# A Strassen-type trunk kernel: the first stage begins with two plain float32 products, and sums, transposes and the end are reordered

## The chip, the cores and the metric

The kernel runs on 1 core of a Trainium2 chip. The metric is the device time of one execution in microseconds (us). The core has five engines that run their own queues in order: TensorE (PE in the rows; its weight loads are PEld), VectorE (DVE), ScalarE (ACT), GpSimd (POOL) and SyncE (SP), which here issues the DMAs. TensorE's clock has two levels, 1.2 and 2.4 GHz; the rows give the granted clock as a share of the higher.

## The reference

One decoder layer on x of 2048 tokens by 1024 features, then a final norm. Cut to what matters:

```
def reference(x, mem, ...):
    x = x + hybrid_mixer(rms_norm(x, g_mix), w_in, ...)          # 1024 -> 3072 columns, attention and short
                                                                 # convolution, norms of both, w_out
    x = x + memory_cross_attention(rms_norm(x, g_xattn), rms_norm(mem, g_mem), ...)
    x = x + squared_relu_mlp(rms_norm(x, g_mlp), w_up, w_down)   # 1024 -> 4096 -> 1024
    return rms_norm(x, g_final)

def rms_norm(x, g):
    return x * rsqrt(mean(x * x, axis=-1) + 1e-6) * g
```

Everything is float32.

## The kernel before

The large products run in stages `g` of 28 steps. A stage multiplies a 1024 x 1024 weight block by 1024 tokens in the scheme of Strassen and Winograd: seven products of 512 x 512 quadrants in the order (1, 2, 6, 7, 4, 5, 3), each in four steps `m`, one for 128 output rows (or, for the values of attention, two steps of 2 x 128 tokens with the operands exchanged). Stage -2 ("vg") is the first: the values and the gate of the first 1024 tokens. Its product 1 is weight quadrant (0,0) by x quadrant (0,0), product 2 is quadrant (0,1) by (1,0); product 6 is the first that needs sums of quadrants.

A product is computed from split operands: ScalarE rounds an operand to float32r (`w_hi` for weights, `o_hi` for activations), VectorE subtracts that from the original (`w_lo`, `o_lo`), and TensorE multiplies high by high, low by high and high by low, three products of 128 x 128 x 512 for each of four k (`mlp_mm`, L370 to L395). In the first stage `o_hi` also scales by `g_mix`, and the row norm is applied to the results. `o_sum` and `w_sum` make the sums of quadrants on VectorE; `x_half` is the scaled x quadrant (0,1) that `o_sum` needs.

The order is written out by hand. Step `n` first evacuates the result of step n-1 (`done`), then issues what `plan` holds for it (`ahead`: roundings, low parts, sums of quadrants), then its products, then what `post` holds (`behind`), then what `later` has due (`tick`). Roundings and low parts are planned up to four steps ahead of the products that use them; `o_at` and `w_at` make exceptions. Every engine takes its instructions in that order. `WHOLE` is a set of products that would run on unsplit operands; it is empty.

Sums over partitions for the norms (`rows`, L105) are products with a column of ones; `rsqrt` turns them into a root on VectorE and ScalarE; `bcast` (L115) broadcasts the result by transposes. They sit at fixed steps: `h_rows` and `h_rb` for the first stages, `conv_rows` for the convolution, `x1_rows` and `x2_rows` for the residuals, `fin_rows` for the last norm. `soft_out` (L1112) evacuates scores and exponentiates, `soft_norm` divides, `soft_t` transposes on TensorE.

The last step is cut into two halves of 256 tokens (`last_mm`); `last_rows`, `last_rb` and `last_out` norm and store them, on VectorE and GpSimd.

Of the kernel before, what the change touches and what calls it, by code (L numbers as in the profile page):

```python
# [50 lines left out]
def _body(tc, a, out):  # L51
# [108 lines left out]
    WHOLE = set()  # L160
# [31 lines left out]
    def w_hi(n):  # L192

        g, r = divmod(n, 28)
        p, m = order[r // 4], r % 4
        if (g, p) in WHOLE:
            return
        src = w_src2(g, p, m)
        if KIND[g] == "vg" and m > 1:
            src = src.rearrange("p m (k c) -> p m k c", k=4)  # L200
            WP[n] = WP[n + 1] = [w4([128, 4, 256], F32R) for l in range(2)]
            hi, lo = (t_.rearrange("p k (m c) -> p m k c", m=2) for t_ in WP[n])
        else:
            WP[n] = WP[n + 1] = [w4([128, 2, 512], F32R) for l in range(2)]
            hi, lo = WP[n]
        if g == -2 and p == 1 and m == 0:
            for j in range(2):
                act.activation(hi[:, j], src[:, j], AF.Copy)
        else:
            act.activation(hi, src, AF.Copy)  # L210
        WP["lo", n] = lo, src, hi

    def w_lo(n):
        if (n // 28, order[n % 28 // 4]) in WHOLE:
            return
        lo, src, hi = WP.pop(("lo", n))
        if n == V0:
            for j in range(2):
                dve.tensor_tensor(lo[:, j], src[:, j], f(hi[:, j]), OP.subtract)
        else:  # L220
            dve.tensor_tensor(lo, src, f(hi), OP.subtract)  # L221
# [39 lines left out]
    def o_src(g, p, k):  # L261
        return o_src2(g, p, k // 2)[:, k % 2]

    def o_hi(o, m):

        g, r = divmod(o, 7)
        p = order[r]
        if (g, p) in WHOLE:
            return
        if m == 0:  # L270
            OP_[o] = [page([128, 4, 512], F32R) for l in range(2)]
        src = o_src2(g, p, m)
        hi, lo = (OP_[o][l][:, 2 * m:2 * m + 2] for l in range(2))
        k0 = {1: 0, 2: 4, 3: 4}.get(p) if g == -2 else None
# [30 lines left out]
    def w_at(n):  # L305
        if W0 <= n < W0 + 4:
            return W0 - 2 + (n - W0) // 2, W0 - 1 + (n - W0) // 2
        if V0 + 8 <= n < V0 + 12:
            return (V0 + 7 + (n - V0 - 8) // 2,) * 2
        return n - LOOK, n - LOOK + 1  # L310

    def o_at(n, m):
        if n == V0:
            return n - 4, n - 4
        if n == V0 + 8:
            return (V0 + 6 + m,) * 2
        return n - 4 + m, n - 3 + m
# [7 lines left out]
    put(V0 + 4, lambda: x_half())  # L325
# [6 lines left out]
    for g in KIND:  # L332
        if KIND[g]:
            for fn, tab in ((w_sum, WSUM[KEEP[g]]), (o_sum, OSUM[KEEP[g]])):
                for i, ds in tab.items():
                    for m, d in enumerate(ds):
                        if g == 6 and i in (2, 3):
                            d = (2, 5)[m] if fn is w_sum else (3, 4)[m]
                        if fn is o_sum and i == 4 and not KEEP[g] and (g, 2) in WHOLE:
                            d += 3  # L340
                        if g == -2 and i in (2, 3):
                            d = (6 if fn is w_sum else 5) + m
                        if g == -2 and fn is o_sum and i == 4:
                            d = 8 + 2 * m
                        put(28 * g + d, fn, g, i, m)
# [201 lines left out]
    for d, fn, j in ((10, h_rows, 0), (11, h_rb, 0), (13, h_rows, 1), (14, h_rb, 1)):  # L547
# [13 lines left out]
    for d, fn, j in ((15, h_rows, 0), (16, h_rb, 0), (24, h_rows, 1), (25, h_rb, 1)):  # L561
# [73 lines left out]
    def conv(hf, j, c):  # L635
# [456 lines left out]
    def res_out(g, p, m, ps):  # L1092
# [4 lines left out]
        if p in DONE:  # L1097
# [4 lines left out]
            if (p, m) in ((4, 3), (3, 3)):  # L1102
                later(3, x1_rows if g < 8 else x2_rows, 2 * t + j, (g, j))
# [8 lines left out]
    def soft_out(g, p, m, ps):  # L1112
# [20 lines left out]
        later(2, soft_t, g, i, j, m, P)  # L1133
# [74 lines left out]
    def final(hf, j):  # L1208
        later(1, fin_rows, hf, j)
# [5 lines left out]
    def down_out(g, p, m, ps):  # L1215
# [4 lines left out]
        if q == 3 and p in DONE:  # L1220
            ys = [m]
            if hf and j and p == 3 and m == 2:
                sq = s2([128, 512])
                act.activation(sq, y, AF.Square)
                acc = acc_["y", 1, 1][:, 0]
                later(1, dve.tensor_tensor, acc, acc, sq, OP.add)
# [115 lines left out]
    bk["st"] = bank()  # L1342
    rv, sq, rbs = ([mk_() for _ in range(2)] for mk_ in (rvec, lambda: s2([128, 256]), lambda: s2([128, 256])))
# [20 lines left out]

    def last_out(h, *work):
        cs = slice(h * 256, h * 256 + 256)
        hs = slice(HT + 512 + h * 256, HT + 768 + h * 256)
        for (i, j), eng in work:
            for m in (2 * j, 2 * j + 1):
                y = Y[1, i, 1][:, m, cs]  # L1370
                if (i, m) == (0, 3):
                    dve.scalar_tensor_tensor(y, y, g_fin[:, 3:4], rbp[h], op0=OP.mult, op1=OP.mult)
                else:
                    eng.tensor_tensor(y, y, rbs[h] if eng is pool else rbp[h], OP.mult)
            k = 4 * i + 2 * j
            sp.dma_start(out[k:k + 2, :, hs].rearrange("k p t -> p k t"), Y[1, i, 1][:, 2 * j:2 * j + 2, cs])
# [89 lines left out]
```

## Time and profile before

| | |
|---|---|
| median of 3 runs | 2710.24 us (2707.25 to 2712.14) |
| profiled execution | 2708.92 us, span 2707.0 us |
| TensorE busy | 2622.8 us, 97% |
| VectorE busy | 2271.1 us, 84% |
| ScalarE busy | 1458.8 us, 54% |
| mean granted clock | 0.983 |

The span runs from the first to the last instruction of the profiled execution; the time of that execution is a little longer. Busy TensorE is not TensorE at its peak: its instructions overlap, and how fast they follow each other is read from a group's busy time over its count.

### The profile page before, as it was taken

What the parts mean: (1) busy time and instruction counts of PE and PEld (TensorE: products, weight loads), DVE (VectorE), ACT (ScalarE), POOL (GpSimd) and SP (SyncE); (2) the same over time, 40 slices, a digit from 0 to 9 for tenths busy, and PEclk for the clock granted to TensorE, in tenths of its full rate; (3) what the DMA queues carried; (4) which work ended last, traced back from release to release, by engine and by line L of the source; (5) the groups of instructions that cost most, each with busy time, mean ns of one, the idle gap of its engine ahead of it and who ended that gap; (6) DMA issues with size and microseconds to landing.
All of it is one profiled execution on the core that took longest, in us unless ns stands there. A gap on an engine that the chain in (4) does not pass through costs nothing.

```text
span 2707.0 us, 35372 instructions
## 1 busy us (share of the span) xinstructions
PE 2622.8 (97%) x13398; PEld 2184.5 (81%) x13398; DVE 2271.1 (84%) x3482; ACT 1458.8 (54%) x2469; POOL 122.7 (5%) x139
## 2 busy tenths in 40 slices
PE   7999999999889999999999999999999999999998
PEld 6888888878778677878788888888887888888887
DVE  7989979768677699988999887879789987978787
ACT  5546545358666344576445637364554636455563
POOL 0000000001444200000000000000000000000000
PEclk9999999999989999999999999999999999999998
DMA  4636444895777945354572311111121511101111
GB/s 157 224 103 207 136 171 139 267 245 128 184 188 223 296 159 169 109 187 156 186 259 100 109 63 63 62 63 58 52 93 48 187 63 63 62 32 49 60 47 62
DMA packets 196683, 353.93 MB, mean 131 GB/s; under 512 B 21025, under 2 KB 76705, under 8 KB 186913
## 3 DMA queue, kind: packets, MB, share of 16 engines
q1 hardware_dynamic: 196512, 351.67, 41.1%
q8 instruction: 106, 1.74, 0.3%
q14 instruction: 65, 0.52, 0.1%
HBM read 264.53 MB, written 87.10 MB: 130 GB/s over the span
## 4 chain that ended last, share of the span: by engine, by line
PE 67%; DVE 20%; DMA 6%; issue 3%; ACT 2%; SPq 1%; POOL 0%; DVEq 0%; ACTq 0%; POOLq 0%
PE ps L391 55%; DVE pg L288 4%; DVE w L221 3%; DMA pg<-qkd 2%; PE ps L854 2%; PE ps L837 2%; PE ps L797 2%; DMA vd<-pg 1%; DVE s L39 1%; PE ps L386 1%; DVE pg L1096 1%; PE ps L798 1%; PE ps L1030 1%; PE ps L1298 1%; PE ps L112 1%
## 5 line engine op out<-in xcount | busy, mean ns | idle before, releaser
L391 PE MATMUL ps<-pg,w 128*128 128x512 f32 x9084 | 2102.7, 393 | 30.1 <-ACT pg L280 11.3
L391 PEld LDWEIGHTS ps<-pg,w 128*128 128x128 f32 x9084 | 1712.1, 189 | 391.0 <-DVE pg L288 14.8
L210 ACT ACTIVATE w<-pg 128x1024 fp32r<-128x1024 f32 x279 | 293.8, 1053 | 279.7 <-PE ps L391 232.0
L221 DVE TENSOR_TENSOR w<-pg,w 128x1024 fp32r<-128x1024 f32 x279 | 342.4, 1227 | 48.7 <-ACT w L210 48.3
L288 DVE TENSOR_TENSOR pg<-pg 128x1024 fp32r<-128x1024 f32 x308 | 374.3, 1216 | 3.3 <-ACT pg L277 2.5
L277 ACT ACTIVATE pg<-pg 128x1024 fp32r<-128x1024 f32 x308 | 313.4, 1045 | 27.2 <-DVE pg L507 13.7
L820 ACT ACTIVATE s<-s,stat 128x256 f32<-128x256 f32 (+1 forms) x384 | 172.6, 451 | 71.5 <-DVE stat L809 70.9
L1219 DVE TENSOR_TENSOR pg<-ps,pg 128x512 f32<-128x512 f32 x223 | 151.8, 684 | 50.1 <-PE ps L391 50.1
L210 ACT ACTIVATE w<-s 128x1024 fp32r<-128x1024 f32 x112 | 117.8, 1052 | 124.9 <-PE ps L391 73.7
L419 ACT ACTIVATE s<-pg 128x1024 f32<-128x1024 f32 x79 | 83.3, 1057 | 184.6 <-DVE pg L1096 116.4
L809 DVE CUSTOM_DVE_ANT_0 s<-ps,w 128x256 f32<-128x256 f32 (+1 forms) x344 | 108.8, 370 | 48.2 <-PE ps L798 42.5
L221 DVE TENSOR_TENSOR w<-s,w 128x1024 fp32r<-128x1024 f32 x112 | 136.0, 1215 | 1.7 <-ACT w L210 1.7
L252 DVE TENSOR_TENSOR pg<-pg 128x1024 f32<-128x1024 f32 x112 | 136.3, 1217 | 1.0
L1190 DVE TENSOR_TENSOR pg<-ps,pg 128x512 f32<-128x512 f32 x96 | 66.0, 687 | 80.7 <-PE ps L391 80.7
L797 PE MATMUL ps<-pg 128*128 128x256 f32 x384 | 108.7, 314 | 9.2 <-DMA pg<-qkd 9.2
L1185 ACT ACTIVATE pg<-ps 128x512 f32<-128x512 f32 x96 | 57.2, 596 | 98.3 <-PE ps L391 97.8
L798 PE MATMUL ps<-pg 128*128 128x256 f32 x384 | 98.6, 288 | 9.6 <-DMA pg<-qkd 9.6
L1191 ACT ACTIVATE pg<-pg 128x512 f32<-128x512 f32 x96 | 60.6, 631 | 80.5 <-DVE pg L1190 80.3
L288 DVE TENSOR_TENSOR pg<-s,pg 128x1024 fp32r<-128x1024 f32 x78 | 94.5, 1219 | 9.7 <-ACT pg L277 9.6
L840 DVE COPY s<-ps 128x256 f32<-128x256 f32 (+1 forms) x192 | 101.0, 566 | 1.3 <-ACT s L820 0.8
L277 ACT ACTIVATE pg<-s 128x1024 fp32r<-128x1024 f32 x78 | 81.9, 1052 | 26.0 <-DVE s L252 25.9
L797 PEld LDWEIGHTS ps<-pg 128*128 128x128 f32 x384 | 74.2, 193 | 25.4 <-issue 14.9
(154 smaller groups left out, 2410.3 us busy)
## 6 DMA issues: line engine op xcount, KB each, us to landing
pg<-w_up SPq DMA_DIRECT2D x32, 1024.0 KB
pg<-w_down SPq DMA_DIRECT2D x32, 1024.0 KB
pg<-qkd SPq DMA_DIRECT2D x44, 512.0 KB
pg<-w_in SPq DMA_DIRECT2D x21, 1024.0 KB
pg<-xT SPq DMA_DIRECT2D x19, 1024.0 KB
qkd<-pg SPq DMA_DIRECT2D x64, 256.0 KB
pg<-x2d SPq DMA_DIRECT2D x16, 1024.0 KB
vd<-pg SPq DMA_DIRECT2D x96, 128.0 KB
```

What stands on the lines that cost most here:

```text
L210: act.activation(hi, src, AF.Copy)
L221: dve.tensor_tensor(lo, src, f(hi), OP.subtract)
L252: dve.tensor_tensor(to, x, y, op)
L277: act.activation(hi, src, AF.Copy)
L288: dve.tensor_tensor(lo, src, f(hi), OP.subtract)
L391: pe.matmul(ps, wt[l][:, m % 2, k * 128:k * 128 + 128], o[x][:, k, cols], start=k == 0 and j == 0 and p in (1, 2, 5), stop=k == 3 and j == ...
L797: pe.matmul(Sh, qv, kv[0], start=True, stop=False)
L798: pe.matmul(Sh, qv, kv[1], start=False, stop=True)
L809: dve.tensor_tensor_reduce(smv, sv, mv, -0.125, 3e38, OP.add, OP.min, mt[:, c1:c1 + 1])
L820: act.activation(pout, pin, AF.Exp, bias=mt[:, c1:c1 + 1], scale=-1.0, accum_out=zt[:, c1:c1 + 1])
L840: dve.tensor_copy(t_.rearrange("p i h q -> p (i h q)")[:, :w], pt[:, :w])
L1219: dve.tensor_tensor(y, ps, y, OP.add)
```

## The change

Products 1 and 2 of the first stage enter `WHOLE`: they run in plain float32 on unsplit operands. `o_hi` for them makes a scaled copy of x in one page; `w_hi`, `w_lo` and `o_lo` do nothing. `x_half` and the sums that product 6 needs move one step earlier. Sums over partitions and broadcasts of `h_rows`, `h_rb`, `conv_rows`, `x1_rows`, `x2_rows`, `fin_rows` (first half), `x_rs` and `x_rb` move to other steps, softmax transposes one step later. At the end the evacuation of the first half-step stands ahead of an add, the sums are cut in two, the scaling is on VectorE alone in wider operations, and two of the stores are issued by ScalarE.

```
-    WHOLE = set()
+    WHOLE = {(-2, 1), (-2, 2)}
...
         if (g, p) in WHOLE:
+            if m == 0:
+                OP_[o] = page([128, 4, 512])
+            for k in (2 * m, 2 * m + 1):
+                gk = g_mix[:, 4 * p - 4 + k:4 * p - 3 + k]
+                act.activation(OP_[o][:, k], XR[p - 1, 0][:, k], AF.Copy, scale=gk)
             return
...
         if V0 + 8 <= n < V0 + 12:
-            return (V0 + 7 + (n - V0 - 8) // 2,) * 2
+            return (V0 + 6 + (n - V0 - 8) // 2,) * 2
...
-    put(V0 + 4, lambda: x_half())
+    put(V0 + 3, lambda: x_half())
...
                         if g == -2 and i in (2, 3):
-                            d = (6 if fn is w_sum else 5) + m
+                            d = (5 if fn is w_sum else 4) + m
...
     def whole_mm(n, p, m, ps):
+        g, x = n // 28, OP_[n // 4]
+        for t in range(2 if m > 1 else 1):
             for k in range(4):
+                if m > 1:
                     b = 2 * m - 4 + t
+                    pe.matmul(ps[:, t * 256:t * 256 + 256].rearrange("p (j c) -> p j c", j=2), x[:, k, b * 128:b * 128 + 128],
+                              WQ[g, 0, p - 1][:, 2:4, k * 128:k * 128 + 128],
+                              start=t == k == 0, stop=k == 3, skip_group_check=True)
+                else:
+                    pe.matmul(ps, w_src(g, p, m)[:, k * 128:k * 128 + 128], x[:, k], start=k == 0, stop=k == 3)
...
-    for d, fn, j in ((10, h_rows, 0), (11, h_rb, 0), (13, h_rows, 1), (14, h_rb, 1)):
+    for d, fn, j in ((10, h_rows, 0), (13, h_rb, 0), (13, h_rows, 1), (16, h_rb, 1)):
...
-    for d, fn, j in ((15, h_rows, 0), (16, h_rb, 0), (24, h_rows, 1), (25, h_rb, 1)):
+    for d, fn, j in ((14, h_rows, 0), (16, h_rb, 0), (23, h_rows, 1), (25, h_rb, 1)):
...
-            later(6, conv_rows, tb)
+            later(9, conv_rows, tb)
...
-                later(3, x1_rows if g < 8 else x2_rows, 2 * t + j, (g, j))
+                later(6, x1_rows if g < 8 else x2_rows, 2 * t + j, (g, j))
...
-        later(2, soft_t, g, i, j, m, P)
+        later(3, soft_t, g, i, j, m, P)
...
-        later(1, fin_rows, hf, j)
+        later(1 if hf else 4, fin_rows, hf, j)
...
+    def last_rows(h):
+        acc = acc_["y", 1, 1]
+        st = bk["st", h] = bank()
+        for i in range(2):
+            for j in range(2):
+                c = 2 * h + j
+                pe.matmul(st[:, j:j + 1], acc[:, i, c * 128:c * 128 + 128], ones, start=i == j == 0, stop=False,
+                          skip_group_check=True)
+    def last_rs(h):
+        st = bk["st", h]
         for j in range(2):
+            pe.matmul(st[:, j:j + 1], sq[h][:, j * 128:j * 128 + 128], ones, start=False, stop=j == 1, skip_group_check=True)
+        rsqrt(rv[h][:, :2], st[:, :2], 2, D)
...
     last_mm(0)
+    acc = acc_["y", 1, 1][:, 0]
+    dve.tensor_tensor(acc, acc, bk["sq"], OP.add)
     last_mm(1, lambda: last_rows(0))
+    last_rs(0)
+    last_rows(1)
     last_rb(0)
-    last_out(0, ((0, 0), dve), ((1, 0), pool))
-    last_rows(1)
+    last_rs(1)
+    last_out(0, ((0, 0), sp), ((1, 0), sp))
     last_rb(1)
-    last_out(0, ((0, 1), dve), ((1, 1), pool))
-    last_out(1, ((0, 0), dve), ((1, 1), pool), ((0, 1), dve), ((1, 0), dve))
+    last_out(0, ((1, 1), sp), ((0, 1), sp))
+    last_out(1, ((0, 0), sp), ((1, 1), act), ((0, 1), sp), ((1, 0), act))
```

The queues show the moves. ScalarE at the start, before (`w_` are rounded weights, `pg` x and its parts, `ps` a result, `s_` squares):

```order
L208 ACTIVATE w_134<-pg 128x512 x2
L280 ACTIVATE pg<-pg,g_mix 128x512 x4
L210 ACTIVATE w_150<-pg 128x2x4x128
L210 ACTIVATE w_154<-pg 128x1024
L280 ACTIVATE pg<-pg,g_mix 128x512 x2
L522 ACTIVATE pg<-ps 128x512
```

and in the changed kernel:

```order
L262 ACTIVATE pg<-pg,g_mix 128x512 x6
L515 ACTIVATE pg<-ps 128x512
L262 ACTIVATE pg<-pg,g_mix 128x512 x2
L515 ACTIVATE pg<-ps 128x512
L412 ACTIVATE s_166<-pg 128x1024
L515 ACTIVATE pg<-ps 128x512
L476 ACTIVATE pg<-pg,g_mix 128x512 x4
```

The roundings of weights are gone, and the scaling of x stands first; L476 is `x_half`.

VectorE at the start, before (L291, L219 and L221 are low parts, L243 `o_sum`, L524 an evacuation):

```order
L291 SCALAR_TENSOR_TENSOR pg<-pg,g_mix 128x512 x4
L219 TENSOR_TENSOR w_135<-pg,w_134 128x512 x2
L221 TENSOR_TENSOR w_151<-pg,w_150 128x2x4x128
L221 TENSOR_TENSOR w_155<-pg,w_154 128x1024
L291 SCALAR_TENSOR_TENSOR pg<-pg,g_mix 128x512 x4
L221 TENSOR_TENSOR w_196<-pg,w_195 128x2x4x128
L39 TENSOR_TENSOR s_225<-s_225,s_254 128x1024
L524 TENSOR_TENSOR pg<-ps,pg 128x512
L243 SCALAR_TENSOR_TENSOR pg<-pg,g_mix 128x512 x4
```

and in the changed kernel (L235 is `o_sum`, L282 a low part of x, L219 and L222 `w_sum`, L213 the low part of its sum):

```order
L39 TENSOR_TENSOR s_166<-s_166,s_183 128x1024
L235 SCALAR_TENSOR_TENSOR pg<-pg,g_mix 128x512 x4
L517 TENSOR_TENSOR pg<-ps,pg 128x512
L282 TENSOR_TENSOR pg<-pg 128x1024
L219 TENSOR_TENSOR pg<-pg 128x1024
L222 TENSOR_TENSOR s_202<-pg 128x1024
L235 SCALAR_TENSOR_TENSOR pg<-pg,g_mix 128x512 x4
L517 TENSOR_TENSOR pg<-ps,pg 128x512
L213 TENSOR_TENSOR w_215<-s_202,w_214 128x1024
```

The low parts of the first two products are gone from the head of the queue, and the sums for product 6 stand ahead of the first evacuation instead of behind it.

TensorE at the end, before, behind the first half of the last half-step (L1357 and L1358 are sums, L119 a broadcast):

```order
L391 MATMUL ps<-pg,w_21221 128x256 x2
L391 MATMUL ps<-pg,w_21222 128x256
L119 MATMUL ps<-ident,rvec 128x128 x2
L1357 MATMUL ps<-ones,s_21217 128x1 x2
L1358 MATMUL ps<-ones,s_21326 128x1
L1357 MATMUL ps<-ones,s_21217 128x1 x2
L1358 MATMUL ps<-ones,s_21326 128x1
L119 MATMUL ps<-ident,rvec 128x128 x2
```

and in the changed kernel (L1349 and L1355 are the sums):

```order
L385 MATMUL ps<-pg,w_21097 128x256 x2
L385 MATMUL ps<-pg,w_21098 128x256
L1355 MATMUL ps<-ones,s_21199 128x1 x2
L1349 MATMUL ps<-ones,s_21093 128x1 x4
L119 MATMUL ps<-ident,rvec 128x128 x2
L1355 MATMUL ps<-ones,s_21200 128x1 x2
L119 MATMUL ps<-ident,rvec 128x128 x2
```

The four sums of the second half now stand ahead of the first broadcast, and two products are left between the two broadcasts.

## Rows read from the trace of the kernel before

**Rows 1.** The page: busy us, share of the span and instructions of each engine.

```profile
PE 2622.8 (97%) x13398; PEld 2184.5 (81%) x13398; DVE 2271.1 (84%) x3482; ACT 1458.8 (54%) x2469; POOL 122.7 (5%) x139
```

**Rows 2.** Stretches of the first stage: length, busy time by engine, clock, DMA.

```profile
core 0: us, PE busy (x) PEld busy (x) DVE busy (x) ACT busy (x) POOL busy (x), PEclk, DMA share, GB/s
22.13:39.30 17.17, 17.13 (x121) 15.96 (x119) 10.36 (x12) 9.38 (x13) 0.00 (x0) 1.00 0.44 143
39.30:44.48 5.18, 0.73 (x2) 0.30 (x2) 5.18 (x8) 2.77 (x3) 0.00 (x0) 0.92 0.65 204
44.48:52.42 7.94, 7.94 (x22) 6.29 (x23) 7.91 (x9) 4.35 (x6) 0.00 (x0) 0.62 0.00 0
```

**Rows 3.** Timeline of the start: start, us, engine, line, operation; in brackets idle before.

```profile
3.48 0.63 ACT L208 ACTIVATE w<-pg 128x512 fp32r<-128x512 f32 x1 [1.24 <-DMA pg<-w_in]
...
9.99 0.63 ACT L208 ACTIVATE w<-pg 128x512 fp32r<-128x512 f32 x1 [5.88 <-DMA pg<-w_in]
...
11.28 1.58 PE L391 MATMUL ps<-pg,w 128*128 128x512 f32 x2 [11.28 <-ACT pg L280]
...
14.66 7.63 PE L391 MATMUL ps<-pg,w 128*128 128x512 f32 x22 [1.79 <-DVE w L219]
...
27.88 5.63 PE L391 MATMUL ps<-pg,w 128*128 128x512 f32 x24
...
28.58 2.55 ACT L483 ACTIVATE pg<-pg,g_mix 128x512 f32<-128x512 f32 x4
...
31.44 2.73 DVE L243 SCALAR_TENSOR_TENSOR pg<-pg,g_mix 128x512 f32<-128x512 f32 x4
...
33.35 5.91 PE L386 MATMUL ps<-w,pg 128*128 128x256 f32 x48
...
43.22 1.21 DVE L221 TENSOR_TENSOR w<-s,w 128x1024 fp32r<-128x1024 f32 x1
```

**Rows 4.** Groups by line: TensorE's products of unsplit float32 operands.

```profile
L1030 PE MATMUL ps<-pg 128*128 128x256 f32 x256 | 56.2, 379 | 0.0
...
L1298 PE MATMUL ps<-pg 128*128 128x512 f32 x64 | 27.9, 593 | 0.0
```

**Rows 5.** TensorE's waits: who, for whom, us in total, times, longest.

```profile
PE ps L112 <- DVE s L39: 11.9, 8, 3.8
...
PE ps L1143 <- DVE pg L1138: 7.8, 8, 1.8
PE ps L119 <- DVE rvec L103: 4.9, 3, 2.4
```

**Rows 6.** Stretches, as in rows 2: plain products, then five sums that wait.

```profile
898.00:927.00 29.00, 29.00 (x83) 14.27 (x82) 17.63 (x27) 13.80 (x20) 4.08 (x2) 1.00 1.01 328
478.00:484.00 6.00, 5.23 (x25) 4.51 (x25) 5.69 (x8) 1.32 (x4) 0.00 (x0) 0.72 0.56 196
1035.00:1047.00 12.00, 8.18 (x31) 6.75 (x30) 11.66 (x14) 5.05 (x6) 0.00 (x0) 0.72 0.85 278
1460.00:1467.00 7.00, 6.66 (x31) 5.35 (x30) 6.97 (x8) 4.38 (x7) 0.00 (x0) 0.76 0.25 93
2050.00:2058.00 8.00, 7.48 (x34) 5.98 (x34) 7.59 (x14) 3.08 (x6) 0.00 (x0) 0.79 0.12 43
2076.00:2085.00 9.00, 7.03 (x32) 5.67 (x31) 8.59 (x15) 5.79 (x9) 0.00 (x0) 0.81 0.01 2
```

**Rows 7.** Timeline behind the sum at 1035: a low part.

```profile
1042.88 1.21 DVE L288 TENSOR_TENSOR pg<-pg 128x1024 fp32r<-128x1024 f32 x1
```

**Rows 8.** Timeline before attention: one load of ScalarE's table.

```profile
580.49 1.28 ACT L1038 ACT_TABLE_LOAD   x1
```

**Rows 9.** Timeline of the end.

```profile
2690.61 0.97 PE L391 MATMUL ps<-pg,w 128*128 128x256 f32 x6 [2.75 <-DVE pg L1349]
...
2697.63 0.16 DVE L97 TENSOR_SCALAR tmp<-ps 128x2 f32<-128x2 f32 x1 [1.10 <-PE ps L1358]
...
2701.86 0.74 DVE L1374 TENSOR_TENSOR pg<-pg,ps 128x256 f32<-128x256 f32 x2
```

More of the change, by code (lines that the diff above doesn't have):

```diff
@@ L205, in w_hi @@
             hi, lo = WP[n]
[L206 to L210, printed above, removed]
+        act.activation(hi, src, AF.Copy)
         WP["lo", n] = lo, src, hi
@@ L216, in w_lo @@
         lo, src, hi = WP.pop(("lo", n))
[L217 to L221, printed above, removed]
+        dve.tensor_tensor(lo, src, f(hi), OP.subtract)
     def w_sum(g, i, m):
@@ L259, in o_src2 @@
         return BQ[g][q][:, 2 * m:2 * m + 2]
-    def o_src(g, p, k):
-        return o_src2(g, p, k // 2)[:, k % 2]
     def o_hi(o, m):
@@ L315, in o_at @@
         if n == V0 + 8:
-            return (V0 + 6 + m,) * 2
+            return (V0 + 5 + m,) * 2
         return n - 4 + m, n - 3 + m
@@ L1224, in down_out @@
                 act.activation(sq, y, AF.Square)
-                acc = acc_["y", 1, 1][:, 0]
-                later(1, dve.tensor_tensor, acc, acc, sq, OP.add)
+                bk["sq"] = sq
             else:
@@ L1260, in _body @@
     XLD = {(0, 0): 4, (1, 0): 6, (1, 1): 12, (0, 1): 13}
-    XSC = {(0, 0): (9, 11, 13, 15), (1, 0): (20, 21, 22, 23), (1, 1): (21, 22, 23, 24), (0, 1): (27, 28, 29, 30)}
+    XSC = {(0, 0): (11, 12, 13, 15), (1, 0): (20, 21, 22, 23), (1, 1): (21, 22, 23, 24), (0, 1): (27, 28, 29, 30)}
     for hf in range(2):
         n = (11 + 8 * hf) * 28
-        after(n + 3, x_rs, hf)
+        after(n + 7, x_rs, hf)
         for q, d in XLD.items():
@@ L1267, in _body @@
         for j in range(2):
-            after(n + 8, x_rb, hf, j)
+            after(n + 10, x_rb, hf, j)
         for (i, j), steps in XSC.items():
@@ L1341, in _body @@
     lt.flush()
-    bk["st"] = bank()
-    rv, sq, rbs = ([mk_() for _ in range(2)] for mk_ in (rvec, lambda: s2([128, 256]), lambda: s2([128, 256])))
+    rv, sq = ([mk_() for _ in range(2)] for mk_ in (rvec, lambda: s2([128, 256])))
     rbp = [None] * 2
@@ L1367, in last_out @@
         hs = slice(HT + 512 + h * 256, HT + 768 + h * 256)
[L1368 to L1374, printed above, removed]
+        for (i, j), q in work:
+            ys = Y[1, i, 1][:, 2 * j:2 * j + 2, cs]
+            if (i, j) == (0, 1):
+                y = Y[1, 0, 1][:, 3, cs]
+                dve.tensor_tensor(Y[1, 0, 1][:, 2, cs], Y[1, 0, 1][:, 2, cs], rbp[h], OP.mult)
+                dve.scalar_tensor_tensor(y, y, g_fin[:, 3:4], rbp[h], op0=OP.mult, op1=OP.mult)
+            else:
+                dve.tensor_tensor(ys, ys, rbp[h].unsqueeze(1).to_broadcast([128, 2, 256]), OP.mult)
             k = 4 * i + 2 * j
-            sp.dma_start(out[k:k + 2, :, hs].rearrange("k p t -> p k t"), Y[1, i, 1][:, 2 * j:2 * j + 2, cs])
+            q.dma_start(out[k:k + 2, :, hs].rearrange("k p t -> p k t"), ys)
     last_mm(0)
+    acc = acc_["y", 1, 1][:, 0]
+    dve.tensor_tensor(acc, acc, bk["sq"], OP.add)
     last_mm(1, lambda: last_rows(0))
+    last_rs(0)
+    last_rows(1)
     last_rb(0)
-    last_out(0, ((0, 0), dve), ((1, 0), pool))
-    last_rows(1)
+    last_rs(1)
+    last_out(0, ((0, 0), sp), ((1, 0), sp))
     last_rb(1)
-    last_out(0, ((0, 1), dve), ((1, 1), pool))
-    last_out(1, ((0, 0), dve), ((1, 1), pool), ((0, 1), dve), ((1, 0), dve))
+    last_out(0, ((1, 1), sp), ((0, 1), sp))
+    last_out(1, ((0, 0), sp), ((1, 1), act), ((0, 1), sp), ((1, 0), act))
     lt.flush()
```

18 lines of the change are left out of this document (1 added, 17 removed).

## The prediction

> **What bounds the kernel now.** I began with the busy shares of the page: TensorE is busy 97% of 2707.0 us, VectorE 84%, ScalarE 54% [rows 1]. So TensorE is the engine to win on, and only through its idle time, its stretches at the lower clock, or its work. Then I cut the first 70 us into stretches [rows 2] and read them in order of time [rows 3]; after that the table of who waited for whom [rows 5], and the granted clock around each wait [rows 6]. The reader should see three things.
>
> First, the start. ScalarE rounds the first weight tile at 3.48, then sits 5.88 us in its queue until the second tile lands at 9.99; only then does it come to the activations, so TensorE starts at 11.28, stops for the missing low parts and goes on at 14.66 [rows 3]. From there it keeps up until 39.3. Second, the third product (order 6): between 39.30 and 44.48 TensorE works 0.73 us, VectorE all 5.18, and in the next 7.94 us the granted clock is 0.62, so 7.94 x 0.38 = 3.0 us are lost to the lower of its two levels, 1.2 GHz [rows 2]. VectorE is the late one: its low part of the summed weights comes at 43.22, 14.6 us after ScalarE began to scale the x quadrant at 28.58 [rows 3]. Third, small waits far apart: sums over partitions wait 11.9 us in 8 places, softmax transposes 7.8 in 8, broadcasts 4.9 in 3 [rows 5], and behind five of the sums the clock falls [rows 6].
>
> **The change part by part.** The sum is made against the profiled execution, 2708.92 us (span 2707.0 and 1.9 around it); the median of the runs shown, 2710.24, is 1.3 above it.
>
> *Two products in plain float32.* Removed: four roundings of weight pairs, and on VectorE four low parts of 1024 columns and eight of 512, 4 x 1.2 + 8 x 0.7 = 10.4 us of its queue. Added: work on TensorE. A plain float32 product with 512 columns takes two records: 64 records of 32 products in 27.9 us, 0.872 us each; with 256 columns 256 records of 128 products in 56.2, 0.439 each [rows 4]. A step is 4 of the first kind or 8 of the second, 3.49 and 3.51 us. Before, two steps took 5.63 (24 products) and 5.91 (48) [rows 3], 2.82 and 2.96 a step. Four steps of each kind: 4 x 0.67 + 4 x 0.55 = 4.9 us more on TensorE.
>
> What comes earlier: nothing stands ahead of the x slices on ScalarE now. The four slices lie between the two weight tiles in the queue, so between 3.48 and 9.99; spread evenly the last lands near 8.7 (estimate). Scaled (0.64, a quarter of 2.55 [rows 3]) and multiplied, the first step ends near 11, its early products at half clock within that wait. The second step's weights are there at 9.99. Seven more steps of 3.5: 35.5, against 39.3. So TensorE passes its dearer work and is 3.8 ahead.
>
> What is late next is VectorE's chain. The scaling of the x quadrant moves one step earlier and starts after the copy of the third step's result, which ends on TensorE at 18: with a square and a copy ahead of it near 20.3 instead of 28.58. A square later VectorE begins, near 23.9, and its order up to the low part for the third product is one add, four and four 512-column operations, two evacuations, three 1024-column operations and the low part: 5 x 1.2 + 10 x 0.7 = 13 us [rows 3], ready near 37.0 (before 44.4). TensorE then waits about 1.1 us from 36.0 instead of 4.5. The second pair follows 6.6 later on VectorE, at 43.6, where before it began at 52.42 [rows 2]: 8.8 earlier. VectorE runs without a pause until the squares for the second sums are added, near 58.4; TensorE wants them at 57.5, so 0.9 goes back, and the 0.7 wait of the first broadcast (part of the 4.9 [rows 5]) is gone. I take **-8.2 us**. If the clock rises only near 16, TensorE arrives at 40 and the gain is 6; if VectorE's chain starts with the quadrant, 10.
>
> *Sums and broadcasts moved.* The stage-one broadcast for the second half now has its sum a step earlier; its 2.4 us (the longest of the three [rows 5]) goes, and VectorE was idle too, waiting for ScalarE's root: **-2.3** (0 to -2.4).
> The convolution's sums stand three steps later. At 478 the wait is 0.77 (6.00 less 5.23 busy), and a clock of 0.72 costs 6 x 0.28 = 1.7 [rows 6]: **-2.2** (0 to -2.5). Of the remaining 11.9 - 7.4 = 4.5 us of sums' waits one part is not touched, and one is the last convolution's, behind which attention waits for casts on VectorE in any case: **-0.5** (-2.5 to +1.5).
> The residual sums stand three steps later. Around 1035 they cost 3.8 idle and 12 x 0.28 = 3.4 of clock [rows 6]. But VectorE is busy 11.66 of these 12 us, and the second half of the next product's low part is only made at 1042.88 to 1044.1 [rows 7]; TensorE would want it near 1040 and stop there instead. Followed on to the product after it, 2.2 remain; with some clock lost, **-1.5** (+0.5 to -4). The like: at 1460 (0.3 idle, 1.7 clock) -1.3, at 2050 and 2076 together (0.5 and 2.0 idle, 1.7 each of clock, VectorE 7.59 of 8 and 8.59 of 9 us busy [rows 6]) **-2.0** (0 to -3.7).
> Softmax transposes come a step later. Behind each on TensorE stands a step of 2.8 us that is ready; the divisions that they wait for are at most 1.8 late [rows 5]. VectorE has pauses in these stages, so most of 7.8 comes out: **-6.0** (-2 to -7.8).
>
> *Root among exponentials.* Two of the moved sums now take their square root between exponentials, so ScalarE loads its table four times more, 1.28 us each [rows 8], 5.1 in its queue. At the start of attention the wait for the sum covers it, in the softmax stage ScalarE is far from full; I take +0.3 (0 to 5.1).
> The Trainium skill (ScalarE: Activation LUTs, Table sets: the hidden batching unit) says to do all exponentials together and then all roots, since each change of set costs a load of about 2.7 us. By that rule and figure the four loads are 10.8 us, and were they on the path the whole sum would be 13.9 instead of 24.4; the trace has 1.28 for one load, so even on the path half of that.
>
> *The end.* The evacuation of the last half-bank no longer stands behind an add that waits for ScalarE; TensorE's 2.75 wait [rows 9] shrinks by 1.3. The second root starts once two products on the last squares are done, not six: near 2695.6 instead of 2697.63. But all scaling is on VectorE, none on GpSimd, and stands behind that second root: 2697.0 plus 8 groups of 0.6 to 0.7 gives 2702.1, where it ended near 2702.6. **-0.7** (-2 to +1.5).
>
> Sum: 8.2 + 2.3 + 2.2 + 0.5 + 1.5 + 1.3 + 2.0 + 6.0 - 0.3 + 0.7 = 24.4; 2684.5 by the profile, 2685.8 by the median: **2686**.
>
> **The rivals.**
> *VectorE gives it back.* VectorE is 95 to 100% busy in the five stretches where sums wait [rows 6]; then taking a wait off TensorE only moves it to the next low part, and only the start, the end and half of the softmax waits stay: 8.2 + 0.7 + 3 = 12, 2698. Against it: at 2.4 us of the broadcast wait and in the softmax stages VectorE itself pauses. 20%.
> *Everything comes back*, each wait with its clock, and 10 at the start: 10 + 2.4 + 2.5 + 2.5 + 4 + 2 + 3.7 + 7.8 + 2 = 37, 2673. Against it: the full VectorE just named. 9%.
> *TensorE stays at 1.2 GHz in the plain products.* Place: steps one to eight, fed slice by slice, and on into the third product. Price: 3.5 us more a step, so eight steps end near 60 where the forecast has 35.5, which alone cancels the gain (2710); if the next product's four steps of 2.9 also take twice as long, as part of them did before at 0.62, 11.6 more: 2722. It decides from the point where the clock has not risen by about 38. Against it: the products of this kind at 898 to 927 ran at a granted 1.00 throughout, TensorE 29.00 of 29 busy [rows 6], and the first stage had 1.00 from 22.13 on [rows 2] although it began with a stop. 4%.
>
> **How the numbers follow.** Forecast 66%, own range 2679 to 2694 (the start 2 either way, softmax 2 to 4, the residual and final sums 3). With the first two rivals the range that should hold the time 8 times in 10 is 2675 to 2701. This measurement can tell about 0.2% (5 us) from no change. Faster by more than that: forecast, both first rivals, 94%. The third rival splits between no change and slower: with a remainder for a term I have not seen, same 3%, slower 3%.
>
> **What would show it.** Right: TensorE's first product near 5 us, plain products of 0.87 at the full clock from about 11, the third product's start near 36 and no clock below 1.0 before 100; no wait at the transposes; a smaller wait for sums, and in its place waits for low parts (the subtractions on VectorE) soon after 1035, 2050 and 2076. A third product that still waits over 3 us would make the start wrong; a wait table where low parts have grown by what sums lost would make the first rival right; matmul spacing of 0.85 us a record in the first 40 us the third.

## The result and the profile after

The changed kernel takes 2687.15 us (median of 6 runs, 2683.34 to 2692.12), the kernel before 2707.83 beside it: ratio 0.9924, 95% interval 0.9909 to 0.9939. In a second set of runs, told below, it took 2683.93 (5 runs), ratio 0.9909 (0.9892 to 0.9926). The forecast was 2686.

The page of the profile after: TensorE's busy time falls by 8.3 us [rows 1], though the plain products added about 4.9 to its work. Busy time also counts what the lower clock stretches, so part of the gain is in it.

```profile
PE 2614.5 (97%) x13350; PEld 2171.2 (81%) x13350; DVE 2259.4 (84%) x3469; ACT 1458.1 (54%) x2466; POOL 116.6 (4%) x133
```

The timeline of its start (start, us, engine, line, operation; in brackets idle before), against [rows 3]. Lines between those shown are left out, here and in the fences below:

```profile
4.79 0.72 ACT L262 ACTIVATE pg<-pg,g_mix 128x512 f32<-128x512 f32 x1 [2.56 <-DMA g_mix<-g_mix]
5.56 9.48 PE L401 MATMUL ps<-pg 128*128 128x512 f32 x16 [5.56 <-ACT pg L262]
14.88 7.07 PE L397 MATMUL ps<-pg 128*128 128x256 f32 x32
19.49 2.55 ACT L476 ACTIVATE pg<-pg,g_mix 128x512 f32<-128x512 f32 x4
21.79 7.03 PE L401 MATMUL ps<-pg 128*128 128x512 f32 x16
24.16 2.73 DVE L235 SCALAR_TENSOR_TENSOR pg<-pg,g_mix 128x512 f32<-128x512 f32 x4
28.66 7.07 PE L397 MATMUL ps<-pg 128*128 128x256 f32 x32
34.80 1.21 DVE L213 TENSOR_TENSOR w<-s,w 128x1024 fp32r<-128x1024 f32 x1
35.37 6.02 PE L385 MATMUL ps<-pg,w 128*128 128x512 f32 x24
42.46 2.78 PE L380 MATMUL ps<-w,pg 128*128 128x256 f32 x21 [0.84 <-DVE w L213]
55.33 0.60 PE L119 MATMUL ps<-ident,rvec 128*128 128x128 f32 x4
56.17 1.22 DVE L39 TENSOR_TENSOR s<-s,s 128x1024 f32<-128x1024 f32 x1
57.53 3.02 PE L112 MATMUL ps<-ones,s 128*128 128x1 f32 x16 [1.60 <-DVE s L39]
```

TensorE starts at 5.56 (before 11.28), two plain steps take 7.03 to 7.07 us, and the third product begins at 35.37 without a wait: the low part (VectorE L213), which its first two matmuls do not need, is made from 34.80 to 36.01. The second pair comes at 42.46, before at 52.42 [rows 2]. Then part of this 10 us goes back, at the second sum over partitions (L112, 57.53).

Five stretches of the same trace (length, busy time by engine, granted clock, DMA share, GB/s), against [rows 2, 6]:

```profile
35.37:41.23 5.86, 5.86 (x26) 4.55 (x25) 5.83 (x7) 2.61 (x3) 0.00 (x0) 1.00 0.56 179
58.11:64.94 6.83, 6.83 (x33) 6.83 (x34) 6.42 (x12) 2.23 (x5) 0.00 (x0) 0.50 0.01 2
477.00:484.00 7.00, 7.00 (x41) 6.05 (x40) 6.59 (x13) 4.19 (x8) 0.00 (x0) 1.00 0.31 112
1026.00:1034.00 8.00, 4.51 (x13) 3.03 (x12) 7.97 (x9) 5.01 (x6) 0.00 (x0) 0.81 1.01 319
1040.00:1340.00 300.00, 299.29 (x1394) 246.77 (x1393) 278.27 (x473) 183.64 (x306) 0.00 (x0) 1.00 0.49 170
```

Behind the second sum the clock is at 0.50, the level of 1.2 GHz, for 6.83 us; at the convolution's sum (477) there is no wait and no fall any more; around 1026 TensorE still idles 3.5 of 8 us while VectorE is full; the softmax stage (1040 to 1340) is almost without a gap.

TensorE's table of waits after, against [rows 5]:

```profile
PE ps L385 <- DVE pg L282: 16.2, 12, 2.9
PE ps L401 <- ACT pg L262: 5.6, 1, 5.6
PE ps L112 <- DVE s L39: 3.2, 2, 1.6
PE ps L119 <- DVE rvec L103: 2.4, 2, 1.5
PE ps L385 <- DVE pg L1183: 2.0, 2, 1.2
```

The waits for sums fall from 11.9 to 3.2 us, those for transposes from 7.8 to nothing over 0.1, those for broadcasts from 4.9 to 2.4. But waits for low parts (L282, which was L288 before) rise to 16.2 us in 12 places, from 9.4 in 7 in the full table before.

### The profile page after: what moved, and what is told of

Its sections match the earlier page's. It is cut to its first block, busy times and chain, and to the rows that moved or that the text cites. A ratio compares the mean times of both kernels' runs of the same rounds, so it can differ in the third digit from the quotient of the medians.

```text
span 2682.8 us, 35255 instructions
## 1 busy us (share of the span) xinstructions
PE 2614.5 (97%) x13350; PEld 2171.2 (81%) x13350; DVE 2259.4 (84%) x3469; ACT 1458.1 (54%) x2466; POOL 116.6 (4%) x133
## 4 chain that ended last, share of the span: by engine, by line
PE 63%; DVE 22%; DMA 9%; issue 3%; ACT 2%; SPq 1%; POOL 1%; DVEq 0%; ACTq 0%; POOLq 0%
PE ps L385 54%; DVE pg L282 4%; DVE w L213 4%; DMA w<-btd 2%; DMA pg<-qkd 2%; PE ps L847 2%; PE ps L380 1%; DVE s L39 1%; PE ps L790 1%; PE ps L830 1%; DVE pg L1089 1%; PE ps L791 1%; DVE pg L244 1%; PE ps L112 1%; DVE pg L219 1%
## 5 line engine op out<-in xcount | busy, mean ns | idle before, releaser
L385 PE MATMUL ps<-pg,w 128*128 128x512 f32 x9036 | 2080.8, 391 | 20.7 <-DVE pg L282 16.2
L385 PEld LDWEIGHTS ps<-pg,w 128*128 128x128 f32 x9036 | 1692.2, 188 | 380.0 <-DVE pg L282 25.0
L282 DVE TENSOR_TENSOR pg<-pg 128x1024 fp32r<-128x1024 f32 x308 | 375.2, 1220 | 3.6 <-ACT pg L271 3.2
L213 DVE TENSOR_TENSOR w<-pg,w 128x1024 fp32r<-128x1024 f32 x276 | 336.5, 1219 | 47.6 <-ACT w L206 47.3
L213 DVE TENSOR_TENSOR w<-s,w 128x1024 fp32r<-128x1024 f32 x112 | 136.1, 1215 | 2.4 <-ACT w L206 2.4
L1183 DVE TENSOR_TENSOR pg<-ps,pg 128x512 f32<-128x512 f32 x96 | 65.9, 687 | 77.6 <-PE ps L385 77.6
L790 PE MATMUL ps<-pg 128*128 128x256 f32 x384 | 108.3, 313 | 10.8 <-DMA pg<-qkd 8.9
L282 DVE TENSOR_TENSOR pg<-s,pg 128x1024 fp32r<-128x1024 f32 x78 | 94.5, 1219 | 9.7 <-ACT pg L271 9.6
```

The costliest lines, as they stand in the source:

```text
L385: pe.matmul(ps, wt[l][:, m % 2, k * 128:k * 128 + 128], o[x][:, k, cols], start=k == 0 and j == 0 and p in (1, 2, 5), stop=k == 3 and j == ...
L790: pe.matmul(Sh, qv, kv[0], start=True, stop=False)
```

## Where the time went, stretch by stretch

The split products with 512 columns are the same in all kernels here, apart from the first two products. Counted from the end, each can be found in two traces, and the difference of its starts says how far a kernel is ahead there. The table shows by how much this grew in each stretch; stretches are given by the time in the first trace of before at which they end, minus is earlier, and the last column is what is left to the end of the span. (2nd is the second half's broadcast, conv. the convolution's sum, att. attention, x1 and x2 the residual sums, soft the softmax stage, fin. the final sums.)

```
stretch        start   2nd        conv  att.    x1  soft    x2        fin.   end
up to            140   300   470   500  1030  1060  1330  1500  2030  2120
before_again    -1.5   0.0  -1.9   0.0  +0.4   0.0  -0.1   0.0   0.0   0.0   0.0
e1_start        -4.9   0.0  +1.6   0.0 -11.8  +1.1  -0.1   0.0   0.0  +1.6  +1.0
e2_soft         -0.6   0.0  -0.4  +1.6  -5.0   0.0  -8.1  -0.8   0.0  +1.6  -0.1
e3_sums         -2.3  -1.6  -0.1  -2.0  -3.6  -1.8  +1.1  -1.1   0.0  -0.9  +1.6
e4_order        -3.9   0.0  -0.5  +1.6  -4.2  -0.2  -0.1   0.0   0.0  +0.1  +0.9
e6_split_early  -1.4   0.0  -0.4   0.0  -2.7  -0.1  -0.1   0.0   0.0   0.0  +0.7
e8_start_rb     -7.4   0.0  +2.4  -1.6  -6.3   0.0  -0.1   0.0   0.0  +0.1  -0.1
after           -6.7  -1.6  +0.1  -2.0  -1.5  -1.6  -7.8  -1.1   0.0  -0.9  -1.0
after_again     -8.0  -1.6  -0.9  -2.0  -7.5  -0.5  -7.8  -1.1   0.0  -0.9  -0.4
e5_rows14       -8.2  -1.6  -0.8  -2.0  -3.5  -1.8  -7.8  -1.1   0.0  -0.9  -0.3
e5_again        -8.2  -1.6  -0.7  -2.0  +0.6  -1.6  -7.7  -1.1   0.0  -0.9  -1.0
e7_load20      -11.1  -1.6  -0.7  -2.0  -0.5  -1.4  -7.8  -1.1   0.0  -0.9  -0.4
e7_again       -10.8  -1.6  +0.1  -2.0  -1.3  -1.6  -7.8  -1.1   0.0  -0.9  -0.4
```

Where a kernel has an edit, the stretch repeats within 0.3 us from trace to trace (second broadcast, softmax, x2, final sums), unless a clock step falls into it. Two stretches do not: the start, by 1 to 2 us, and attention, by many. The end was not run alone, but all six traces that have its edit lie between -0.3 and -1.0 there, and the seven other traces between -0.1 and +1.6.

## The experiments

Each ratio is to the kernel before, run beside.

**The parts alone.** e1_start is the kernel before with the changed start:

```diff
-    WHOLE = set()
+    WHOLE = {(-2, 1), (-2, 2)}
...
-    put(V0 + 4, lambda: x_half())
+    put(V0 + 3, lambda: x_half())
```

> The kernel before with the changed start alone (two products in plain float32, the x quadrant scaled and the sums of the first stage made one step earlier); the moved sums, broadcasts, transposes and the end stay as before. My theory is that the parts of the change add up, each worth what its own stretch of the changed kernel's trace shows. There TensorE stands 6.7 us earlier at 130 us, 0.6 of it from the first broadcast's wait, which here remains: about 6.1 us earlier from 130 us to the end, 2707.8 - 6.1 = 2701.7 us; the third product starts near 35.4, and the granted clock falls once behind the second sum near 58. The rival, VectorE gives it back: at 130 us TensorE is less than 3 us earlier, above 2705.

Measured: 2697.88 us, 0.9972 (0.9961 to 0.9983). In the trace it is 11.7 ahead at 60, but 5.6 at 100 and 4.9 at 140, since the first broadcast, at its old step, became a wait of 4.01 us (0.7 at this place before), with the lower clock behind it; the 7.8 us of its median hold more, as its trace does in attention. From its timeline:

```profile
34.89 6.02 PE L385 MATMUL ps<-pg,w 128*128 128x512 f32 x24
53.55 0.75 PE L119 MATMUL ps<-ident,rvec 128*128 128x128 f32 x4 [4.01 <-DVE rvec L103]
```

So half of the start's gain is gone at the first broadcast. The clock fell once here, at 53.98, not near 58.

e8_start_rb adds that one line to e1_start:

```diff
-    for d, fn, j in ((10, h_rows, 0), (11, h_rb, 0), (13, h_rows, 1), (14, h_rb, 1)):
+    for d, fn, j in ((10, h_rows, 0), (13, h_rb, 0), (13, h_rows, 1), (16, h_rb, 1)):
```

> The kernel before with the changed start and the two broadcasts of the first stage at their new steps (13 and 16 instead of 11 and 14), nothing else. With the start alone TensorE waited 4.01 us for the first broadcast and stood 4.9 us earlier at 140. My theory: the moved broadcast keeps what that wait took, 6.7 to 8.0 us earlier at 140 as in the two traces of the changed kernel, with a wait of about 1.6 us for the second sum instead and a granted clock of 0.50 behind it. The rival: the clock's loss behind the second sum takes all of it, 5 us earlier at 140 as with the start alone. In the whole time 2 us more or less will not show beside the spread of attention.

Measured: 2695.81 us, 0.9959 (0.9944 to 0.9974); 7.4 ahead at 140, a wait of 1.6 for the second sum and the clock at 0.50 from 58.09 to 64.92, as the theory had it. But it too is 11.6 ahead at 60 and 6.7 at 100: the moved broadcast costs nothing, and the second sum takes nearly as much. Of the 2.5 us between the two at 140, 1.1 stand at 100; the rest comes with a wait of 1.35 us for a low part near 126, which only e1_start has. Each is one trace.

e2_soft is the kernel before with the transposes one step later:

```diff
-        later(2, soft_t, g, i, j, m, P)
+        later(3, soft_t, g, i, j, m, P)
```

> The kernel before with the softmax transposes one step later and nothing else. My theory: all eight waits go (7.8 us) and nothing else comes late, 2700.0 us; TensorE stands 7.8 us earlier from 1320 us on. My prediction had 6.0 for this (2701.8). The rival, VectorE gives it back: half of it returns as waits for low parts, 2704.

Measured: 2698.23 us, 0.9977 (0.9965 to 0.999). 8.1 come out in the softmax stretch. TensorE's one wait in that stretch (1060 to 1330), where eight were:

```profile
PE ps L391 <- DVE pg L288: 0.5, 1, 0.5
```

e3_sums has only the moved sums and broadcasts, for instance:

```diff
-            later(6, conv_rows, tb)
+            later(9, conv_rows, tb)
...
-                later(3, x1_rows if g < 8 else x2_rows, 2 * t + j, (g, j))
+                later(6, x1_rows if g < 8 else x2_rows, 2 * t + j, (g, j))
```

> The kernel before with the moved sums and broadcasts alone (h_rows, h_rb, conv_rows, x1_rows and x2_rows, x_rs, x_rb and the scaling behind them, fin_rows). My theory, by the stretches of the changed kernel's trace: 0.6 (first broadcast) + 1.6 (second half's broadcast) + 2.0 (convolution) + 1.4 (attention and what follows) + 1.7 and 1.1 (residual sums) + 0.8 (final sums) = 9.2 us, 2698.6. The rival, VectorE gives it back: waits for low parts grow by most of what the sums lose, about 4 us remain, 2704. Four table loads more on ScalarE (5.1 us of its queue) cost nothing by mine; if they were on the path they would show as waits for ScalarE, up to 5 us.

Measured: 2701.86 us, 0.9987 (0.9977 to 0.9998): 3.8 us by the medians where 9.2 were expected and the rival had about 4. In its trace the stretches do give 1.6 + 2.0 + 1.8 + 1.1 + 0.9 = 7.4 as in the changed kernel, but waits move where the rival said. TensorE's table:

```profile
PE ps L391 <- DVE pg L288: 14.8, 12, 2.9
PE ps L1143 <- DVE pg L1138: 8.8, 8, 1.8
PE ps L119 <- DVE rvec L103: 2.6, 2, 1.8
```

The waits for low parts are 14.8 us in 12 places (9.4 in 7 before). What is gained at the first residual sum is clock: 3.49 us of idle at 1028 to 1036 (3.8 before [rows 5]), but 3.4 us at the lower level instead of 6.8. Of the 7.4, 1.1 go back in the softmax stretch, where the transposes at their old step wait 8.8 us instead of 7.8 (see the table loads below), and 1.6 at the end, where the clock falls 18.7 us before the end of the span instead of 14.6. That leaves 4.7, near what the 12 runs give, which spread from 2695.79 to 2707.62. In time the rival was right here.

By the medians, e8_start_rb gives 10.4, e2_soft 7.5 and e3_sums 3.8 us, together 21.7 (the moved broadcasts of the first stage are in two of them); the whole change gave 20.7 and 25.2.

**Are the plain products needed?** e4_order keeps all products split and changes ScalarE's queue: the second tile is rounded behind the x slices.

```diff
-            for j in range(2):
-                act.activation(hi[:, j], src[:, j], AF.Copy)
+            act.activation(hi[:, 0], src[:, 0], AF.Copy)
...
                 put(o_at(n, m)[0], o_hi, n // 4, m)
+        if n == V0:
+            put(V0 - 4, lambda: act.activation(WP["lo", V0][2][:, 1], WP["lo", V0][1][:, 1], AF.Copy))
```

> The kernel before with one edit: ScalarE scales and rounds the four x slices ahead of the second weight tile, so TensorE can start on the first step before that tile is there; all products stay split, and the sums stay in their steps. My theory: TensorE starts near 5.6 as in the changed kernel and finishes its first eight steps near 32, but the third product waits for VectorE, whose 10.4 us of low parts stay in its queue; about 3 us are gained, 2705. The rival, the order in ScalarE's queue is all that the start gained: 6 us or more, 2702 or less, and the plain products are not needed.

e6_split_early has this and the one-step-earlier chain of the change (`x_half`, the sums, `w_at`, `o_at`).

> The kernel before with all products split, ScalarE's order at the start as in the run that changed that order alone, and the x quadrant, the sums and the rounding for the third product one step earlier, as in the change. It leaves only the plain float32 products out of the changed start. My theory: VectorE's low parts for the first two products (10.4 us) still stand ahead of the chain, so the third product waits about 2.5 us until 37.5 (35.4 with plain products, 40.2 with the order alone) and about 4.5 us are gained over the kernel before, 2701. Rival: the plain products are not needed, the third product starts by 35.5 and the gain equals that of the changed start alone (7.8 us, 2698). The other rival: the chain gains nothing by starting earlier, 2703 as with the order alone.

Measured: 2703.01 us, 0.9992 (0.9981 to 1.0002), and 2705.81 us, 0.9997 (0.9986 to 1.0009). Neither can be told from no change. TensorE in e4_order, then in e6_split_early:

```profile
5.33 1.58 PE L392 MATMUL ps<-pg,w 128*128 128x512 f32 x2 [5.33 <-ACT pg L279]
10.56 7.43 PE L392 MATMUL ps<-pg,w 128*128 128x512 f32 x22 [3.64 <-DVE w L218]
35.81 0.73 PE L392 MATMUL ps<-pg,w 128*128 128x512 f32 x2 [0.86 <-ACT w L209]
40.19 5.06 PE L392 MATMUL ps<-pg,w 128*128 128x512 f32 x11 [3.64 <-DVE w L220]
```

```profile
35.30 0.73 PE L392 MATMUL ps<-pg,w 128*128 128x512 f32 x2 [0.44 <-ACT w L209]
38.53 6.75 PE L392 MATMUL ps<-pg,w 128*128 128x512 f32 x22 [2.50 <-DVE w L220]
56.49 0.90 PE L119 MATMUL ps<-ident,rvec 128*128 128x128 f32 x3 [3.68 <-DVE rvec L103]
```

An early start alone only lengthens the wait for VectorE: split products need their low parts at once (in e4_order 3.64 from 6.92), and the third product waits again, 3.64 or 2.50. I had expected 4.5 us from e6_split_early; I had not counted that its first broadcast, at the old step as in e1_start, takes 3.68 and the clock after it. e1_start carries the same burden and is faster by 0.25%, with intervals that do not meet: the plain products pay, at about 4.9 us more on TensorE. That they do so by taking work off VectorE is read from the waits: both that e1_start is rid of were for its low parts (2.89 until 11.01 and 2.50 until 38.53 in e6_split_early).

**Why the clock fell behind the second sum.** e5_rows14 is the changed kernel with one number more:

```diff
-    for d, fn, j in ((10, h_rows, 0), (13, h_rb, 0), (13, h_rows, 1), (16, h_rb, 1)):
+    for d, fn, j in ((10, h_rows, 0), (13, h_rb, 0), (14, h_rows, 1), (16, h_rb, 1)):
```

> The changed kernel with one number more: the second sum of the first stage (h_rows of the second half) stands at step 14 instead of 13. In the changed kernel TensorE waits 1.60 us for it at 55.93, and from 58.11 to 64.94 the granted clock is 0.50. My theory: the wait lowered the clock, so both go, 1.6 + 3.2 = 4.8 us, 2682.4 us; the clock stays at 1.00 up to 100 us. Rival one: the sixteen products of one column themselves lower the clock, then only 1.6 us go, 2685.5, and the clock still falls behind them. Rival two, VectorE gives it back: the product that follows waits for its low part instead, no change, 2687.

> The changed kernel with the second sum at step 14, again, to set it against the changed kernel in the same call. My theory: 2 to 5 us faster than the changed kernel (2683), the clock at 1.00 until attention; between 100 and 140 us 3.8 of 5.3 us are given back to a weight tile that lands late. The rival, the difference so far was spread of executions: equal to the changed kernel within 1 us.

> The changed kernel, unchanged, again, on the same chip as the two that follow. 2687 us, ratio 0.992; with the second sum of the first stage at step 13 the clock falls near 58 again. If its position behind attention (990 us) differs from its first trace by some us with equal waits before 500 us, the rest is spread of attention from one execution to the next.

Measured: 2682.78 us, 0.9916 (0.9898 to 0.9935), and again 2682.98, 0.9903 (0.9888 to 0.9918); the changed kernel in that second set 2683.93, 0.9909. The stretch of the second sum in e5_rows14, and where the gain goes next:

```profile
55.00:65.00 10.00, 9.86 (x76) 9.29 (x75) 9.59 (x16) 6.78 (x13) 0.00 (x0) 1.00 0.01 2
102.00:110.00 8.00, 7.27 (x33) 5.70 (x32) 4.39 (x6) 4.42 (x7) 0.00 (x0) 1.00 0.64 227
119.00:124.00 5.00, 2.96 (x13) 2.15 (x12) 5.00 (x6) 2.95 (x3) 0.00 (x0) 1.00 0.38 125
```

The sixteen products of one column are still there, the wait is not, and the clock stays at 1.00: without the wait they do not lower it. A wait as such need not lower it either: in the last row TensorE waits 2.04 us in one piece, and the clock is 1.00. In time the gain is not shown: beside each other the two took 2682.98 and 2683.93, 0.95 us apart, as the rival of the second run had it (within 1 us) and not my 2 to 5. At 100 us this kernel is 5.3 ahead of the changed one; at 140 only 1.5. At 102 to 110 VectorE itself pauses 3.6 of 8 us, and ScalarE shows why, a rounding that waits for a weight tile:

```profile
105.58 1.06 ACT L206 ACTIVATE w<-pg 128x1024 fp32r<-128x1024 f32 x1 [8.07 <-DMA pg<-w_in]
```

e7_load20 keeps the second sum at step 14 and issues this load two steps earlier, ahead of twelve stores on SyncE's queue:

```diff
-            for d, q in ((13, (0, 0)), (19, (1, 1)), (21, (1, 0)), (22, (0, 1))):
+            for d, q in ((13, (0, 0)), (19, (1, 1)), (20 if g == -2 else 22, (0, 1)), (21, (1, 0))):
```

> The changed kernel with the second sum at step 14 and, in the first stage, the load of the next stage's second weight tile issued at step 20 instead of 22, ahead of twelve stores of values on SyncE's queue. My theory: with the sum at 14 TensorE waits 0.73, 0.38 and 2.04 us at 108 to 121 because ScalarE rounds this tile only at 105.6, when it has landed; with the earlier load those 3.2 us go, 2680. The rival: the load waits in the queue for its page all the same, or the tile behind it lands later by as much, no gain.

> The changed kernel with the second sum at step 14 and the weight tile loaded at step 20, again. If its gain over the changed kernel is real: 2680 us, ratio near 0.990, 11.1 us earlier than the kernel before at 140, and no wait above 1 us between 60 and 260. If the first result was a lucky draw of attention: 2683 to 2686.

Measured: 2680.02 us, 0.9892 (0.9874 to 0.991), and again 2678.83, 0.9894 (0.988 to 0.9907). The rounding begins at 97.78; the waits of 0.7, 0.4 and 2.0 become one of 0.5 (1.0 in the second trace), and the kernel is 11.1 ahead at 140 (10.8). All its 8 runs (2676.88 to 2683.31) lie below the median of the changed kernel's 11 (2685.65), and their median is some 6 us below it. Beside each other the medians of e7_load20 and the changed kernel were 3.9 apart (4 and 5 runs, which overlap), and the intervals of the ratios overlap too, so a gain over the change is likely but its size is open.

**How much of a trace is spread.** before_again is the kernel before, once more.

> The kernel before, unchanged, profiled a second time. Between the positions of 500 and 990 us (attention) the five other traces stand 1.5 to 13 us earlier against the first trace of before than the edits explain. If these are differences from one execution to the next, this trace differs there from the first one by some us too, with equal waits in the first 500 us and behind 1050; if the edits make them, the two traces agree there within 0.5 us.

Measured: one time, 2705.97 us. It agreed in attention (+0.4) and differed at the start. The second trace of the changed kernel settles what this one left open: with equal code, attention gave 1.5 us in one trace and 7.5 in the other, and in the two traces of e5_rows14's code 3.5 and, the other way, 0.6. What is gained ahead of attention can be lost in it and come back: before_again stood 3.4 ahead at 540, waited 1.62 and 5.90 us there for a tile of `w_qT` (3.01 in the first trace), was 0.4 behind at 580 and 3.2 ahead again at 880. So a trace shows what an edit does in its own stretch, and only the runs show the sum.

## Why the prediction was right, and where its steps were not

Its sum of 24.4 us stands against 24.2 from span to span, and 20.7 and 25.2 by the medians of the two sets. Part of that agreement is luck: the stretches with an edit give 6.7 + 1.6 + 2.0 + 1.6 + 7.8 + 1.1 + 0.9 + 1.0 = 22.7, and the rest is attention. Among these terms, too, 1.8 more than forecast at the softmax transposes make up for 1.5 less at the start and 1.1 less at the final sums.

*Two products in plain float32* (8.2): 6.7, 8.0 in the second trace. Right: the start at 5.56, 3.5 us a step, ScalarE's scaling at 19.49 (20.3 forecast), VectorE's chain from 24.16 (23.9), no sign of the third rival from about 10 us on. The low part was ready at 36.0 instead of 37.0, and since only the third matmul of the step wants it, the forecast wait of 1.1 us did not come. The step that failed is "so 0.9 goes back" at the second sums: 1.60 us of wait, and behind it 6.83 us at half the clock (3.42 in the second trace), which I had not priced, although [rows 6] show five sums with a wait and just such a fall. The sign "no clock below 1.0 before 100" was thereby wrong. Nor did I see that the first broadcast, booked at 0.7, would take 6.0 us of the start at its old step (e1_start is 11.7 ahead at 60 and 5.6 at 100).

*Second half's broadcast* (2.3): 1.6. Its 2.4 us of wait went, but the low parts wanted at 271 and 286 are waited for 2.32 and 1.65 us, 1.0 more than before (1.29 and 1.66).

*The convolution's sums* (2.2): 2.0, the wait and the clock both. The last one (0.5) cannot be separated from the spread of attention.

*Residual sums* (1.5 and 1.3): 1.6 and 1.1. As forecast, the wait does not go: 3.82 us for the sum became 0.58 + 2.91 for low parts, and what is saved is clock.

*Final sums* (2.0): 0.9. Waits grew here, from 0.52 + 1.97 to 1.11 + 0.71 + 0.34 + 1.19, with TensorE held up by evacuations on VectorE (L1183); only the clock came back. Here "VectorE gives it back" was right.

*Softmax transposes* (6.0): 7.8, all of the eight waits. I had held back a quarter for VectorE, busy 278 of 300 us there in the trace after; its pauses were enough.

*Table loads* (0.3): there are nine instead of five, 1.28 us each, and in the changed kernel TensorE waits for none of them. Two of the groups by line after, the loads ahead of the roots (L98) and ahead of the exponentials (L1123): busy, mean ns, idle before.

```profile
L98 ACT ACT_TABLE_LOAD x4 | 5.1, 1283 | 0.1
L1123 ACT ACT_TABLE_LOAD x2 | 2.6, 1283 | 5.2 <-DVE small L1121 5.2
```

The Trainium skill (ScalarE: Activation LUTs, Table sets: the hidden batching unit) would have exponentials and roots each done together. The change does the opposite in two places and loses nothing that the changed kernel's traces show, since ScalarE is not what TensorE waits for there. Its 2.7 us for a switch is not seen as busy time: the row has 1.28. In e3_sums, with the transposes at their old step, the moved root is not free. Behind it and its two loads (at 1122.16 and 1126.82) the first transposes wait 1.59 and 0.98 us, where they waited 0.91 and 0.55 before. How much of these 1.1 us is the loads, and how much the root's own chain on VectorE, is not separated; the later transposes cover both.

*The end* (0.7): 1.0 and 0.4 in the two traces. The wait ahead of the last half-step is 1.35 instead of 2.75 [rows 9], and two waits for roots, 0.90 and 1.48, stand where one of 1.76 stood. The scaling ends at 2678.29, in the last row:

```profile
2666.02 0.97 PE L385 MATMUL ps<-pg,w 128*128 128x256 f32 x6 [1.35 <-DVE pg L1340]
2671.09 0.40 PE L119 MATMUL ps<-ident,rvec 128*128 128x128 f32 x2 [0.90 <-DVE rvec L103]
2673.31 0.69 PE L119 MATMUL ps<-ident,rvec 128*128 128x128 f32 x2 [1.48 <-DVE rvec L103]
2677.61 0.68 DVE L1371 TENSOR_TENSOR pg<-pg,ps 128x512 f32<-128x512 f32 x1
```

Last, the rivals. The first, VectorE gives it back, is what the waits for low parts show at 271, 1028 and 2047; it took nothing in the softmax stage. In the first trace it took back waits and hardly any clock, but at 271 the second trace has 3.41 us at the lower level as well. Everything comes back, the second, was not seen: its 2673 needed these waits to go too. In the chances, 66, 20 and 9 make 95, not 94.

## What to carry to other kernels

Where the busiest engine waits for a late one, taking work off the late one can pay even if it adds work to the busiest: the plain products cost TensorE about 4.9 us and shortened VectorE's queue by 10.4. After each gain, look at the next fixed point behind it (a broadcast, a sum, a weight load, each at a step written down by hand) and move that too: here, in the traces, each one in turn held part of the gain until it was moved. And price a short wait on TensorE together with the clock that may fall behind it.

## What was not expected of the hardware

A wait of 1.60 us was enough to put TensorE at 1.2 GHz for 6.83 us in one execution and 3.42 in another of the same code (and for 6.83 in e8_start_rb); without it the clock did not fall in any of four traces. But the same wait does not always bring a fall. Ahead of the convolution's sum, seven traces with that sum at its old step have a wait of 0.77 to 0.79 us; behind it the clock is at the lower level for 3.41 us in four of them, for 6.83 in two, and not at all in one. The two rows are before and e8_start_rb:

```profile
477.00:485.00 8.00, 7.23 (x33) 5.88 (x32) 7.59 (x13) 3.32 (x7) 0.00 (x0) 0.79 0.54 178
472.00:480.00 8.00, 7.23 (x40) 5.98 (x39) 7.59 (x13) 3.32 (x7) 0.00 (x0) 1.00 0.54 178
```

So one trace with a fall, or without, does not price a wait. And in the trace after the clock column says 1.00 from the first instant, but the weight loads of the plain products stood 0.85 us apart until about 10 and 0.43 from there:

```profile
8.28 0.34 PEld L401 LDWEIGHTS ps<-pg 128*128 128x128 f32 x1 [0.52 <-ACT pg L262]
9.14 0.34 PEld L401 LDWEIGHTS ps<-pg 128*128 128x128 f32 x1 [0.52 <-issue]
11.02 0.19 PEld L401 LDWEIGHTS ps<-pg 128*128 128x128 f32 x1 [0.24 <-issue]
11.45 0.19 PEld L401 LDWEIGHTS ps<-pg 128*128 128x128 f32 x1 [0.24 <-issue]
```

That is the ratio of the two levels; so the spacing of the instructions, not that column, tells the level at the start here. The trace's first record of the clock, at 1.00, begins only at 10.32; the column reads 1.00 ahead of it too. In the eight traces with plain products this record begins at 8.7 to 11.1, in the six others, which stop for low parts first, at 14.4 to 19.8 (before: 19.76). An earlier full clock may thus be a part of the start's gain; no run shows how large.
